# One wide operand for the high and low parts of the tokens in the single-stream projections

## The chip, the cores and the metric

The kernel runs on one core of a Trainium2 chip, in one launch. The metric is the device time of that core in microseconds (us), the median of several executions. Engines: PE is TensorE (PEld its weight loads), DVE is VectorE, ACT is ScalarE, POOL is GpSimd, SP is SyncE, which issues most of the DMAs.

## The reference

One layer of a hybrid block over 256 latent tokens and 256 context tokens, model width 2048, all in float32. What matters here are the matrix products of the latent tokens alone:

```python
hl = modulate(rmsnorm(x_lat, norm_mix[l]), m_lat[0], m_lat[1])
pl = hl @ w_in[l]                      # columns U, V, P, Q, O, K, VM, G
ql = silu(centred_dwconv(pl[Q]))       # 3 taps along the tokens, per channel
h_l = mlstm_bidir(ql, kl, vl, gl, ctx_states)            # 4 heads, 2 directions
y_b = sigmoid(pl[O]) * (rmsnorm of h_l * mlstm_norm)
y_a = gelu(pl[U]) * (spatial gating of gelu(pl[V]))
x_lat = x_lat + m_lat[2] * (concat(y_a, y_b, y_c) @ w_out[l])
hf = modulate(rmsnorm(x_lat, norm_ffn[l]), m_lat[3], m_lat[4])
q = hf @ peer_wq[l]                    # scores against keys, top 16, then the expert tables
x_lat = x_lat + m_lat[5] * peer_ffn(hf, ...)
out = rmsnorm(x_lat, norm_final)
```

The context tokens only pass through the columns K, VM and G.

## The kernel before

**Products in three parts.** A float32 weight tile `raw` is split in two: ACT copies it to `hi` in the rounded type fp32r (L282), and DVE takes the rest, `lo = raw - hi` (L292). The tokens are split in the same way, part 0 high and part 1 low, in the tiles `xL` (latent), `xC` (context), `ysplit` and `hf`. A product is hi x high + hi x low + lo x high, three matmuls into one PSUM tile.

**Units.** Weights come in units of 128 x 1024 (512 KB), half of a projection of 128 output channels. Each unit takes 8 of the 16 slices k of the model width (`add_cm`, L475). For one stream of 256 tokens that is 24 matmuls a unit, in the order (hi, 0), (hi, 1), (lo, 0) for every k, each with 256 columns. There are 52 such projections with one stream, 104 units, 832 slices: 8 of q, 8 of o, 4 of u, 16 of w_out and 16 of wq. K and the gates (two streams) and VM, V and P (`add_tm`, 512 columns) are made in other ways. Later, the 256 units of the table u_t (`u_use`, L323) pass `hA`, 192 tokens with high and low side by side, as one operand of 384 columns, then lo with 192.

**Order.** Everything is issued in program order by a planner in the kernel: `step` (L356) takes the next unit; `prepare` issues loads, `hi` and `lo` as far as slots are free (3 tiles of hi, 3 of lo); `flush` issues the evacuation (`q_done`, `o_done`, `u_done`, `o2_done`, `q2_done`) of the projection that ended one unit earlier; then come the unit's own matmuls. After the fourth k of a unit and after the unit, `pump` lets side work advance whose due time on a rough clock has come: lane "main" (states `gen_C` with the PSUM tile pc, then `gen_heads`), lane "score", and others. For lane "main" the due time also depends on the kernel's estimates of how far DVE and ACT have come. Each engine works off its own instructions in the order issued.

**Evacuation.** `conv_silu` (L677) for q: ACT copies PSUM to x, ACT scales it by the middle tap into y, DVE adds the two outer taps (two `scalar_tensor_tensor`, written big<-big,vecs 128x255), ACT does Silu and a last scaling. `o_done` and `u_done` read PSUM with one ACT activation; `o2_done` reads it with one DVE `scalar_tensor_tensor` onto the residual `x1`; `q2_done` with one ACT copy. Between units DVE also sums the condition's weights (`ada_use`, L434, adacc, 1024 columns).

**Heads.** For each head and direction, `weights` needs a broadcast from PE (bc), DVE (big<-bc, qw, sT) and an ACT Exp; `products` needs sT on PE (num, den); then den, diag, PE all, ACT E, and so on.

Of the kernel before, what the change touches and what calls it, by code (L numbers as in the profile page):

```python
# [32 lines left out]
P = 128  # L33
D = 2048
KD = D // P
T = 256
# [137 lines left out]
def build(tc, a, stack, dbg=None):  # L174
# [294 lines left out]
                add(a["ada2"][g - 2, part, k], False, ada_use(g, part, k))  # L469


    xL = A.tile([P, 2, KD, T], F32R, name="xL", tag="xL")
    xC = A.tile([P, 2, KD, T], F32R, name="xC", tag="xC")

    def add_cm(src, streams, done, n_ada=0):  # L475


        box = {}

        def use(half):  # L480
            def f(u):
                if half == 0:
                    box["ps"] = mm_ps()
                ps = box["ps"]
                xs = streams() if callable(streams) else streams
                hi = u.hi.rearrange("p (k c) -> p k c", c=P)
                lo = u.lo.rearrange("p (k c) -> p k c", c=P)
                for kt in range(8):
                    k = half * 8 + kt
                    for w, part in ((hi, 0), (hi, 1), (lo, 0)):  # L490
                        for n, x in enumerate(xs):
                            mm(ps[:, n * T:(n + 1) * T], w[:, kt], x[:, part, k],
                               start=(k == 0 and w is hi and part == 0 and n == 0),
                               stop=(k == KD - 1 and w is lo and n == len(xs) - 1))
                    if kt in MID:
                        pump()
                if half == 1:
                    post.append(lambda: done(ps))
            return f

        def put(half):
            add(src[:, half], True, use(half))
            add_ada(n_ada)
        return put
# [169 lines left out]
        yield 2.0  # L674


    def conv_silu(ps, ch, n):  # L677
        x, y = big()[:, 0:n], big()[:, 0:n]
        act.activation(x.rearrange("p n t -> p (n t)"), ps[:, 0:n * T], AF.Copy)

        def w(j):
            return vecs[:, V_CONV + j * 16 + ch:V_CONV + j * 16 + ch + 1]

        act.activation(y, x, AF.Copy, scale=w(1))
        vec.scalar_tensor_tensor(y[:, :, 1:], x[:, :, :T - 1], w(0), y[:, :, 1:], op0=OP.mult, op1=OP.add)
        vec.scalar_tensor_tensor(y[:, :, :T - 1], x[:, :, 1:], w(2), y[:, :, :T - 1], op0=OP.mult, op1=OP.add)
        return y
# [63 lines left out]
    def o_done(c):  # L751
        def f(ps):

            act.activation(V["yb"][:, c], ps[:, 0:T], AF.Sigmoid)
            act.activation(V["yb"][:, c], V["yb"][:, c], AF.Copy, scale=vecs[:, V_MLN + c:V_MLN + c + 1])
            V["o"] = c
        return f
# [186 lines left out]

    def u_done(c):
        def f(ps):
            act.activation(V["ya"][:, c], ps[:, 0:T], GELU)
            drain(only=("sgu",))
            ya = V["ya"][:, c].rearrange("p (b t) -> p b t", b=2)
            vec.tensor_tensor(ya, ya, mx[c], op=OP.mult)  # L950
        return f
# [23 lines left out]
    def finish_mix(u):  # L975
        drain(only=("main", "sgu", "pool"))
        dump("ya", V["ya"])
        dump("yb", V["yb"])
        dump("yc", V["yc"])
        y = Y["y"] = A.tile([P, 2, KD, T], F32R, name="ysplit", tag="xL")  # L980

        def v(k):
            q, c = divmod(k, 4)
            return (V["yc"][:, c], V["yb"][:, c], V["ya"][:, c], V["yb"][:, 4 + c])[q]

        skew(KD, lambda k: act.activation(y[:, 0, k], v(k), AF.Copy),
             lambda k: vec.tensor_tensor(y[:, 1, k], v(k), y[:, 0, k].bitcast(F32), op=OP.subtract))
        Y["x"] = A.tile([P, KD, T], F32, name="x1", tag="xc")
        load_x(0)
# [5 lines left out]
    def o2_done(c):  # L995
        def f(ps):
            x1 = Y["x"]
            vec.scalar_tensor_tensor(x1[:, c], ps[:, 0:T], mod[:, 2, 0, c:c + 1], x1[:, c],
                                     op0=OP.mult, op1=OP.add)
            if c % 4 == 0 and c + 4 < KD:  # L1000
                load_x(c // 4 + 1)
            sq = V["B"].tile([P, T], F32, name="sq1", tag="kc", bufs=2)
            act.activation(sq, x1[:, c], AF.Square)
            if c == KD - 1:

                warm = V["B"].tile([P, 1], F32, name="warm")
                act.activation(warm, ones[:, 0:1], AF.Sqrt)
                Y["last"] = sq
                return

            if c == 0:
                Y["sq"] = V["B"].tile([P, T], F32, name="sqs", tag="E")
            late.append(lambda: vec.tensor_copy(Y["sq"], sq) if c == 0 else
                        vec.tensor_tensor(Y["sq"], Y["sq"], sq, op=OP.add))
        return f
# [8 lines left out]
    def make_hf(u):  # L1024
        drain(only=("ada",))
        x1 = Y["x"]
        ss = mm_ps("ss1")
        mm(ss[:, 0:T], ones, Y["sq"], start=True, stop=False)
        mm(ss[:, 0:T], ones, Y["last"], start=False, stop=True)
        prepare()  # L1030
        rs = con.tile([P, T], F32, name="rs1", tag="rs1")
        rstd_of(rs, ss[:, 0:T], D)
        araws.drop(V["B"])
        close_pool(V["pb"])
        R["rh"] = open_pool("rh", side="right")
        R["rsb"] = open_pool("rsb", side="right")
        R["rs"] = open_pool("rs", side="right")
        H, S, SB = R["rh"][1], R["rs"][1], R["rsb"][1]
        hA = H.tile([P, KD, 2, NA], F32R, name="hA", tag="hA")
        hB = H.tile([P, D], F32, name="hB", tag="hB")  # L1040
        hf = A.tile([P, 2, KD, T], F32R, name="hf", tag="xC")
        R.update(hA=hA, hB=hB, hf=hf)
        R["keys"] = S.tile([P, 2, NK], F32, name="keys")
        sync.dma_start(R["keys"], a["keys"])
        sync.dma_start(x1d, x1)
        dump("x1", x1)
        n2 = 2 * PH * TOPK
        R["val"] = SB.tile([P, 2, n2], F32, name="val")
        R["ix"] = SB.tile([P, 2, n2], U32, name="ix")
        R["s0"] = SB.tile([P, 2 * PH, NK], F32, name="s0")  # L1050
        R["sc"] = SB.tile([P, PH, TOPK], F32, name="sc")
        R["ci"] = SB.tile([P, PH, TOPK], U32, name="ci")
        R["e12"] = SB.tile([P, 3, PH, TOPK], F32, name="e12")
        late = A.tile([P, 8192], F32, name="late", tag="xL")
        h32 = R["h32"] = late[:, 0:4096].rearrange("p (k t) -> p k t", t=T)
        R["scr"] = late[:, 4096:]
        spawn("hA", copy_hA())
        shift = mod[:, 3, 0]
        skew(KD,
             lambda k: vec.scalar_tensor_tensor(h32[:, k], x1[:, k], gm[:, 2, k:k + 1], rs,  # L1060
                                                op0=OP.mult, op1=OP.mult),
             lambda k: act.activation(hf[:, 0, k], h32[:, k], AF.Identity, bias=shift[:, k:k + 1]),
             lambda k: vec.scalar_tensor_tensor(hf[:, 1, k], h32[:, k], shift[:, k:k + 1],
                                                hf[:, 0, k].bitcast(F32), op0=OP.add, op1=OP.subtract))
        dump("hf", hf.bitcast(F32))

    hBd = tc.dram_tile([P, D], F32, name="hB_spill")

# [107 lines left out]
    def q2_done(hp):  # L1176
        def f(ps):
            S = R["rs"][1]
            at_most(1, "score")
            q = S.tile([P, T], F32, name="q2", tag="q2", bufs=2)  # L1180
            act.activation(q, ps[:, 0:T], AF.Copy)

            def g():
                yield 2.0
                pk = sm_ps("sc")
                for blk in range(2):
                    mm(pk[:, blk * P:(blk + 1) * P], q[:, blk * P:(blk + 1) * P], R["keys"][:, hp % 2],
                       start=True, stop=True)
                s = S.tile([P, NK], F32, name="s", tag="s", bufs=4)
                act.activation(s, pk[:, P:T], AF.Copy)  # L1190
                act.activation(R["s0"][:, hp], pk[:, 0:P], AF.Copy)
                R[hp] = s
                yield 1.5
                if hp % 2:
                    score_top(1, (hp - 1, R.pop(hp - 1)), (hp, R.pop(hp)))
                yield 0.0
                if hp % 4 == 3:
                    pair_top(1, hp // 2 - 1)
                    yield 0.0
                if hp == LOOK_AT:  # L1200
                    spawn("look", gen_look(1, 0, LOOK_Y))
            spawn("score", g())
        return f
# [523 lines left out]
```

## Time and profile before

| | |
|---|---|
| median of 3 executions | 1967.14 us (1966.36 to 1968.19) |
| profiled execution | 1964.81 us, span 1962.7 us |
| PE, PEld busy | 1727.7 us (88%), 1366.7 us (70%) |
| DVE, ACT busy | 1227.2 us (63%), 709.0 us (36%) |
| mean granted TensorE clock | 0.944 |
| HBM | 340 GB/s over the span |

Times in rows are microseconds from the start of the span. In the timeline, a matmul's first number is its start and the second its duration with the pipeline's filling and draining, so the distance between starts, not the duration, tells the pace. By the starts of the rows, the stages are: products with two streams to 183, VM to 281, q 283 to 337, o, V, P, o and u from 339 to 523 with the heads between them, w_out 532 to 630, wq 637 to 752, the table u_t from 753 on, and then the gathered rows of the table v.

### The profile page before, as it was taken

How to read it: one execution, taken by the hardware profiler on the slowest of the kernel's cores; microseconds unless marked ns; L12 is line 12 of the kernel's file. 1: busy time of each engine (PE TensorE's matmuls, PEld its weight loads, DVE VectorE, ACT ScalarE, POOL GpSimd, SP SyncE). 2: the span in 40 equal slices, each digit the busy share in tenths (PEclk: the TensorE clock that was granted, in tenths of full speed). 3: DMA queues.
4: the chain of work that ended last, by engine and by line, in shares of the span. 5: the costliest groups of instructions: out<-in, count | busy, mean ns of one | idle time of the engine just before them, and what ended most of it. 6: DMA issues, size and time to landing. Idle time of an engine off the chain costs nothing.

```text
span 1962.7 us, 30021 instructions
## 1 busy us (share of the span) xinstructions
PE 1727.7 (88%) x11882; PEld 1366.7 (70%) x11882; DVE 1227.2 (63%) x2504; ACT 709.0 (36%) x1131; POOL 376.1 (19%) x324
## 2 busy tenths in 40 slices
PE   4999999999898999899899999999987776767775
PEld 2689789979798998899789888888753222222221
DVE  5256868776798669899689998664434323323232
ACT  4236335555544654454434444444421001001010
POOL 0000000000000000333222323113333333333331
PEclk8999999999899999999999999999988889888887
DMA  9975878776598455999999999989989999999996
GB/s 397 375 268 181 289 245 305 273 250 205 197 348 291 150 177 197 409 420 420 418 350 406 396 395 393 357 343 408 377 345 421 421 420 421 420 421 422 420 421 288
DMA packets 115869, 670.20 MB, mean 341 GB/s; under 512 B 12688, under 2 KB 15248, under 8 KB 53264
## 3 DMA queue, kind: packets, MB, share of 16 engines
q1 hardware_dynamic: 69648, 332.72, 45.5%
q0 software_dynamic: 46080, 335.56, 41.8%
q8 instruction: 93, 1.52, 0.3%
q14 instruction: 48, 0.39, 0.1%
HBM read 662.99 MB, written 5.24 MB: 340 GB/s over the span
## 4 chain that ended last, share of the span: by engine, by line
PE 60%; DMA 26%; issue 5%; DVE 5%; ACT 2%; POOL 1%; SPq 0%; POOLq 0%; ACTq 0%; DVEq 0%
PE mm L345 25%; PE ups L345 22%; DMA gath<-in_v_rows,eA 7%; DMA rawB<-in_v_rows,eA 4%; DMA raw<-in_v_rows,eA 3%; PE adaps L345 3%; DMA hB<-in_v_rows,eA 2%; PE y L345 2%; DMA ring<-in_ada 2%; DMA rawB<-in_u_t 2%; DVE lo L130 2%; DMA rawA<-in_v_rows,eA 2%; PE sm L345 1%; PE num L345 1%; PE yb L345 1%
## 5 line engine op out<-in xcount | busy, mean ns | idle before, releaser
L345 PE MATMUL ups<-hA,hi 128*128 128x384 f32 x2048 | 607.2, 368 | 3.4 <-ACT hi L130 3.4
L345 PE MATMUL ups<-hA,lo 128*128 128x192 f32 x2048 | 518.8, 253 | 22.6 <-DVE lo L130 21.9
L345 PEld LDWEIGHTS ups<-hA,hi 128*128 128x128 f32 x2048 | 389.8, 190 | 53.3 <-issue 43.6
L345 PEld LDWEIGHTS ups<-hA,lo 128*128 128x128 f32 x2048 | 396.6, 194 | 27.6 <-DVE lo L130 27.4
L130 DVE TENSOR_TENSOR lo<-rawA,hi 128x1024 fp32r<-128x1024 f32 x158 | 192.7, 1221 | 120.8 <-ACT hi L130 106.0
L130 DVE TENSOR_TENSOR lo<-rawB,hi 128x1024 fp32r<-128x1024 f32 x156 | 190.3, 1221 | 116.3 <-ACT hi L130 108.3
L130 DVE SCALAR_TENSOR_TENSOR px<-c,iT,pick 128x128 f32<-128x128 f32 x192 | 55.3, 344 | 298.4 <-PE pick L345 289.8
L130 ACT ACTIVATE hi<-rawA 128x1024 fp32r<-128x1024 f32 x158 | 166.8, 1056 | 189.9 <-PE ups L345 91.3
L130 ACT ACTIVATE hi<-rawB 128x1024 fp32r<-128x1024 f32 x156 | 164.6, 1056 | 171.3 <-PE ups L345 68.4
L1351 POOL DMA_INDIRECT W<-in_u_rows,idx x30 | 48.7, 1623 | 894.2 <-PE ups L345 782.7
L345 PE MATMUL mm<-xL,hi 128*128 128x256 f32 x864 | 181.6, 290 | 4.8 <-ACT xL L130 1.7
L345 PEld LDWEIGHTS mm<-xL,hi 128*128 128x128 f32 x864 | 144.5, 193 | 14.2 <-issue 7.5
L130 DVE SCALAR_TENSOR_TENSOR adacc<-araw,early,adacc 128x1024 f32<-128x1024 f32 x120 | 152.3, 1277 | 0.0
L345 PE MATMUL y<-gath,wA 128*32 128x512 f32 x648 | 102.6, 720 | 53.2 <-DMA gath<-in_v_rows,eA 52.8
L130 ACT ACTIVATE uA<-uA 128x4 f32<-128x4 f32 x48 | 9.9, 206 | 385.8 <-DVE px L130 385.8
L130 ACT ACTIVATE hi<-W 128x1024 fp32r<-128x1024 f32 x82 | 86.9, 1059 | 107.3 <-PE ups L345 90.3
L345 PE MATMUL mm<-xL,lo 128*128 128x256 f32 x432 | 122.7, 284 | 0.0
L345 PEld LDWEIGHTS pick<-W,oh 128*128 128x128 f32 x384 | 79.7, 258 | 57.7 <-issue 56.2
L130 DVE TENSOR_TENSOR lo<-W,hi 128x1024 fp32r<-128x1024 f32 x82 | 99.4, 1218 | 15.2 <-ACT hi L130 13.5
L1351 POOL DMA_INDIRECT gath<-in_v_rows,idx x48 | 71.0, 1480 | 184.4 <-PE yb L345 90.4
L345 PE MATMUL mm<-hf,hi 128*128 128x256 f32 x512 | 100.0, 295 | 6.1 <-ACT hf L130 5.2
L1351 POOL DMA_INDIRECT gath<-in_v_rows,eA x81 | 76.6, 945 | 136.3 <-PE y L345 122.4
(291 smaller groups left out, 2985.2 us busy)
## 6 DMA issues: line engine op xcount, KB each, us to landing
araw<-in_ada SPq DMA_DIRECT2D x128, 512.0 KB, 5.3
W<-in_u_t SPq DMA_DIRECT2D x41, 1024.0 KB, 10.3
rawB<-in_u_t SPq DMA_DIRECT2D x40, 1024.0 KB, 11.3
rawA<-in_u_t SPq DMA_DIRECT2D x40, 1024.0 KB, 7.9
ring<-in_ada SPq DMA_DIRECT2D x32, 1024.0 KB, 11.8
rawB<-in_wout SPq DMA_DIRECT2D x16, 512.0 KB, 6.8
rawA<-in_wout SPq DMA_DIRECT2D x16, 512.0 KB, 5.7
rawB<-in_wq SPq DMA_DIRECT2D x16, 512.0 KB, 3.8
```

Of the source, the lines that this page charges most:

```text
L130: return f(*args, **kw)
L345: ten.matmul(out, lhsT, rhs, start=start, stop=stop, skip_group_check=True, **kw)
L1351: pool.indirect_dma_start(out=g.raw, out_offset=None, in_=tab, in_offset=bass.IndirectOffsetOnAxis(ap=idx, axis=0))
```

## The change

The token tiles `xL`, `ysplit` and `hf` now hold high and low of a slice k side by side. Where `add_cm` has one stream, hi is multiplied with both parts in one matmul of 512 columns, whose halves go to the two halves of the PSUM tile, and lo with the high part into the first half. The two halves are added when the tile is evacuated: `total` copies the second half on ACT and adds the first on DVE. q, o, u and wq use `total`; w_out adds each half onto the residual in an instruction of its own.

```diff
-    xL = A.tile([P, 2, KD, T], F32R, name="xL", tag="xL")
+    xL = A.tile([P, KD, 2, T], F32R, name="xL", tag="xL").rearrange("p k s t -> p s k t")
...
-                    for w, part in ((hi, 0), (hi, 1), (lo, 0)):
+                    if len(xs) == 1:
+                        mm(ps.rearrange("p (s t) -> p s t", s=2), hi[:, kt], xs[0][:, :, k], start=(k == 0), stop=False)
+                        mm(ps[:, 0:T], lo[:, kt], xs[0][:, 0, k], start=False, stop=(k == KD - 1))
+                    for w, part in ((hi, 0), (hi, 1), (lo, 0)) if len(xs) > 1 else ():
...
+    def total(dst, ps):
+        act.activation(dst, ps[:, T:2 * T], AF.Copy)
+        vec.tensor_tensor(dst, dst, ps[:, 0:T], op=OP.add)
+
     def conv_silu(ps, ch, n):
         x, y = big()[:, 0:n], big()[:, 0:n]
-        act.activation(x.rearrange("p n t -> p (n t)"), ps[:, 0:n * T], AF.Copy)
+        if n == 1:
+            total(x[:, 0], ps)
+        else:
+            act.activation(x.rearrange("p n t -> p (n t)"), ps[:, 0:n * T], AF.Copy)
...
-            act.activation(V["yb"][:, c], ps[:, 0:T], AF.Sigmoid)
+            total(V["yb"][:, c], ps)
+            act.activation(V["yb"][:, c], V["yb"][:, c], AF.Sigmoid)
...
-            act.activation(V["ya"][:, c], ps[:, 0:T], GELU)
+            total(V["ya"][:, c], ps)
+            act.activation(V["ya"][:, c], V["ya"][:, c], GELU)
...
-            vec.scalar_tensor_tensor(x1[:, c], ps[:, 0:T], mod[:, 2, 0, c:c + 1], x1[:, c],
-                                     op0=OP.mult, op1=OP.add)
+            for part in range(2):
+                vec.scalar_tensor_tensor(x1[:, c], ps[:, part * T:(part + 1) * T], mod[:, 2, 0, c:c + 1], x1[:, c],
+                                         op0=OP.mult, op1=OP.add)
...
-            act.activation(q, ps[:, 0:T], AF.Copy)
+            total(q, ps)
```

`ysplit` and `hf` change their layout as `xL` does.

On DVE, in the stage of q, this is the place of one projection's evacuation (big<-big,mm is the add of `total`, big<-big,vecs x2 the two outer taps, lo the next unit's weights):

```order
-L130 TENSOR_TENSOR lo_2431<-rawB,hi_2429 128x1024
+L130 TENSOR_TENSOR lo_2415<-rawB,hi_2413 128x1024
+L130 TENSOR_TENSOR big<-big,mm 128x256
 L130 SCALAR_TENSOR_TENSOR big<-big,vecs 128x255 x2
 L130 SCALAR_TENSOR_TENSOR adacc<-araw_2307,early,adacc 128x1024
 L130 COPY early<-pc 128x1 x2
```

The add stands between lo and the taps, and ACT's scaling of its result stands between the add and the taps.

On ACT, in the same stage, the evacuation of a state (b_1025<-pc) and the next units' hi; big<-big is the Silu, b_2361 the finished q:

```order
-L130 ACTIVATE hi_2719<-rawA 128x1024
-L130 ACTIVATE b_1025<-pc 128x256 x2
-L130 ACTIVATE hi_2761<-rawB 128x1024
+L130 ACTIVATE hi_2651<-rawA 128x1024
+L130 ACTIVATE hi_2675<-rawB 128x1024
 L130 ACTIVATE big<-mm 128x256
 L130 ACTIVATE big<-big,vecs 128x256
 L130 ACTIVATE big<-big 128x256
 L130 ACTIVATE b_2361<-big 128x256
-L130 ACTIVATE hi_2807<-rawB 128x1024
-L130 ACTIVATE hi_2839<-rawA 128x1024
+L130 ACTIVATE b_1025<-pc 128x256 x2
+L130 ACTIVATE hi_2719<-rawB 128x1024
+L130 ACTIVATE hi_2748<-rawA 128x1024
```

The copies of pc have moved from behind a hi to ahead of the next one; this happens twice in the stage.

On DVE, after the last projection of q, the weights of the first head (big<-bc, qw, sT):

```order
 L130 STREAM_TRANSPOSE adatr<-adat 128x256
 L130 TENSOR_TENSOR mod<-adatr,vecs 128x8
 L130 SCALAR_TENSOR_TENSOR gm<-mod,vecs 128x8
-L130 SCALAR_TENSOR_TENSOR big<-bc_3053,early 128x128
-L130 TENSOR_SCALAR big<-bc_3053,early 128x128
-L130 SCALAR_TENSOR_TENSOR big<-bc_3053,early 128x128
-L130 TENSOR_TENSOR qw<-b_2361,bc_3053 128x256 x2
+L130 TENSOR_TENSOR lo_2927<-rawA,hi_2925 128x1024
+L130 SCALAR_TENSOR_TENSOR adacc<-araw_2789,early,adacc 128x1024
+L130 SCALAR_TENSOR_TENSOR big<-bc_2941,early 128x128
+L130 TENSOR_SCALAR big<-bc_2941,early 128x128
+L130 SCALAR_TENSOR_TENSOR big<-bc_2941,early 128x128
+L130 TENSOR_TENSOR qw<-b_2361,bc_2941 128x256 x2
 L130 TENSOR_TENSOR sT<-big,S 128x256
 L130 TENSOR_TENSOR sT<-big,S 128x128
```

A lo and an adacc that stood behind sT now stand ahead of big<-bc. On PE, the first products num stand three units after the last unit of q, where they stood two and a half units after it.

## Rows read from the trace of the kernel before

**Rows 1.** The page's chain that ended last, by engine.
```profile
PE 60%; DMA 26%; issue 5%; DVE 5%; ACT 2%; POOL 1%; SPq 0%; POOLq 0%; ACTq 0%; DVEq 0%
```

**Rows 2.** Busy time by windows (length, engines, clock, DMA share, GB/s): q, w_out, wq.
```profile
281.00:343.00 62.00, 60.37 (x468) 57.36 (x467) 52.97 (x80) 36.50 (x64) 0.00 (x0) 1.00 0.84 291
...
532.00:631.00 99.00, 97.37 (x797) 95.44 (x798) 89.11 (x113) 42.58 (x63) 0.00 (x0) 0.97 0.82 304
637.00:753.00 116.00, 114.31 (x1085) 109.33 (x1085) 82.80 (x274) 65.45 (x133) 0.00 (x0) 0.97 0.47 161
```

**Rows 3.** Timeline (start, duration) of PE in w_out, 256 columns.
```profile
576.34 0.28 PE L345 MATMUL mm<-ysplit,lo 128*128 128x256 f32 x1
...
576.70 0.28 PE L345 MATMUL mm<-ysplit,lo 128*128 128x256 f32 x1
```

**Rows 4.** Timeline of PE in VM, 512 columns, first and last of 19.
```profile
209.84 0.39 PE L345 MATMUL mm<-hi,xC 128*128 128x512 f32 x1
...
213.92 0.39 PE L345 MATMUL mm<-hi,xL 128*128 128x512 f32 x1
```

**Rows 5.** Timeline of PE in u_t, 384 and 192 columns by turns.
```profile
757.18 0.36 PE L345 MATMUL ups<-hA,hi 128*128 128x384 f32 x1
757.38 0.25 PE L345 MATMUL ups<-hA,lo 128*128 128x192 f32 x1
757.47 0.36 PE L345 MATMUL ups<-hA,hi 128*128 128x384 f32 x1
```

**Rows 6.** Timeline of DVE in q; idle time and its releaser in brackets.
```profile
296.37 1.23 DVE L130 TENSOR_TENSOR lo<-rawB,hi 128x1024 fp32r<-128x1024 f32 x1 [0.79 <-ACT hi L130]
...
314.51 1.00 DVE L130 SCALAR_TENSOR_TENSOR big<-big,vecs 128x255 f32<-128x255 f32 x2
...
317.45 1.22 DVE L130 TENSOR_TENSOR lo<-rawA,hi 128x1024 fp32r<-128x1024 f32 x1 [0.74 <-ACT hi L130]
...
336.61 1.23 DVE L130 TENSOR_TENSOR lo<-rawB,hi 128x1024 fp32r<-128x1024 f32 x1 [0.75 <-ACT hi L130]
```

**Rows 7.** Timeline of ACT around the same projection of q.
```profile
312.05 0.51 ACT L130 ACTIVATE big<-big,vecs 128x256 f32<-128x256 f32 x1
315.60 0.42 ACT L130 ACTIVATE big<-big 128x256 f32<-128x256 f32 x1 [3.04 <-DVE big L130]
...
316.38 1.04 ACT L130 ACTIVATE hi<-rawA 128x1024 fp32r<-128x1024 f32 x1
```

**Rows 8.** Groups by form: a DVE tensor_tensor of 256 columns from PSUM.
```profile
L130 DVE TENSOR_TENSOR qw<-b,bc 128x256 f32<-128x256 f32 x16 | 5.9, 411 | 0.0
```

**Rows 9.** Timeline of DVE and PE at the first head.
```profile
343.73 0.35 DVE L130 SCALAR_TENSOR_TENSOR big<-bc,early 128x128 f32<-128x128 f32 x1 [0.69 <-PE bc L345]
...
345.18 0.62 DVE L130 TENSOR_TENSOR sT<-big,S 128x256 f32<-128x256 f32 x2
...
348.04 0.82 PE L345 MATMUL num<-sT,vlat 128*128 128x256 f32 x4
```

**Rows 10.** Timeline of ACT near the third head's norm.
```profile
486.96 1.28 ACT L130 ACT_TABLE_LOAD   x1
...
489.12 0.69 ACT L130 ACTIVATE diag<-c,hrs 128x128 f32<-128x128 f32 x2 [0.23 <-DVE hrs L130]
```

**Rows 11.** Timeline of PE there, and at the end of u.
```profile
489.70 0.66 PE L345 MATMUL all<-diag,ones 128*128 128x128 f32 x4
...
528.75 1.87 PE L345 MATMUL hss<-ones,h 128*128 128x1 f32 x8 [5.41 <-ACT h L130]
```

**Rows 12.** Timeline of DVE in w_out.
```profile
590.29 1.23 DVE L130 TENSOR_TENSOR lo<-rawB,hi 128x1024 fp32r<-128x1024 f32 x1 [0.28 <-ACT hi L130]
591.43 0.48 DVE L130 SCALAR_TENSOR_TENSOR x<-mm,mod,x 128x256 f32<-128x256 f32 x1
591.82 1.28 DVE L130 SCALAR_TENSOR_TENSOR adacc<-araw,early,adacc 128x1024 f32<-128x1024 f32 x1
```

**Rows 13.** Timeline of DVE and PE near the end of wq.
```profile
742.73 1.22 DVE L130 TENSOR_TENSOR lo<-rawA,hi 128x1024 fp32r<-128x1024 f32 x1
...
744.15 0.60 PE L345 MATMUL sc<-keys,q 128*128 128x128 f32 x4
```

**Rows 14.** Busy time by windows, around the end of u.
```profile
525.00:550.00 25.00, 18.50 (x125) 18.13 (x126) 18.71 (x34) 12.26 (x26) 0.00 (x0) 0.80 0.51 160
```

More of the change, by code (lines that the diff above doesn't have):

```diff
@@ L979, in finish_mix @@
         dump("yc", V["yc"])
-        y = Y["y"] = A.tile([P, 2, KD, T], F32R, name="ysplit", tag="xL")
+        y = Y["y"] = A.tile([P, KD, 2, T], F32R, name="ysplit", tag="xL").rearrange("p k s t -> p s k t")
         def v(k):
@@ L1040, in make_hf @@
         hB = H.tile([P, D], F32, name="hB", tag="hB")
-        hf = A.tile([P, 2, KD, T], F32R, name="hf", tag="xC")
+        hf = A.tile([P, KD, 2, T], F32R, name="hf", tag="xC").rearrange("p k s t -> p s k t")
         R.update(hA=hA, hB=hB, hf=hf)
@@ L1064, in make_hf @@
                                                 hf[:, 0, k].bitcast(F32), op0=OP.add, op1=OP.subtract))
-        dump("hf", hf.bitcast(F32))
+        dump("hf", hf)
     hBd = tc.dram_tile([P, D], F32, name="hB_spill")
```

## The prediction

> **What bounds the kernel now.** I read the chain of waits first: it runs over PE for most of the span and over DMA for the gathered rows at the end [rows 1]. The changed stages lie in front of that, so I went to the busy time by windows: in q, w_out and wq PE is busy nearly throughout at full clock, and DMA has room [rows 2]. So the pace of PE's matmuls counts there, as long as DVE and ACT keep up. DVE is close: 52.97 of 62.00 us in q and 89.11 of 99.00 in w_out. Then I read the timeline, where the distance between starts is the pace. Three matmuls of 256 columns take 0.36 us, 120 ns each [rows 3]; 18 steps of 512 columns take 4.08 us, 226.7 ns each [rows 4]. At 2.4 GHz the columns alone would need 106.7 and 213.3 ns, so every matmul costs 13.3 ns besides its columns.
>
> **PE.** A slice took 3 x 120 = 360 ns and will take 226.7 + 120 = 346.7: 13.3 ns less, 0.107 us a unit, 11.1 us over 832 slices. The neighbours are the pairs of 384 and 192 columns in u_t, 0.29 us a pair [rows 5], where 576 columns and two times 13.3 would be 267 ns; 20 ns are unexplained. If that is a price of alternating lengths, a slice costs 367 ns, 7 more than before. If it is because the load of the next weights outlasts the stream of 192 columns (80 ns), it vanishes here, since 256 columns take longer; the pair then lasts 340 to 347 ns. I take 346.7, with 340 and 367 as ends.
> The Trainium skill (TensorE: Matmul & The Clock Gate, section Back-to-back issue gap) gives columns / 2.4 + 2.5 ns for a matmul at full clock. By it a slice would gain 2.5 ns, and the sum below would be about 10.6 instead of 3.5. The trace's 13.3 ns decides. The same page (section LDWEIGHTS) puts a load of 128 columns at columns / 1.2, an estimated 107 ns; that is longer than 80 ns and supports the second reading of rows 5, and no row here separates the two.
>
> **q, 283 to 337.** Here PE is not alone. After the taps of one projection (314.51, done 315.5) ACT does Silu (315.60), the last scaling, and only then the next hi (316.38); DVE's lo waits for that hi, idle 0.74 us, until 317.45 [rows 6, 7]. That hi did not wait for PE. DVE and ACT form a ring whose time is spent on these two engines alone: from 296.37 to 336.61 it made 6 rounds, 6.71 us each [rows 6], which is also PE's pace (48 x 0.12 = 5.76 plus the matmuls of the states). In the round ACT's scaling by the middle tap is hidden: it ran at 312.05 to 312.56, two us before the taps [rows 7]. With the change it can't be. DVE's add stands between lo and the taps, and the scaling needs the add: 0.41 for the add [rows 8], 0.10 until ACT starts (as from 315.50 to 315.60), 0.51 for the scaling, 0.04 back: 1.06 us a round. The ring then needs 7.8 us where PE needs 6.5, so DVE and ACT set the pace. Over 8 projections that is 8.5 us. The copies of pc, 0.64 us, now stand ahead of a hi in two rounds and lengthen them: about 1.4. So the last taps come 9.9 us late. Next, a lo (1.14) and an adacc (1.19) have moved ahead of the first head's weights; they take the 0.69 us that DVE idled there and wait about half a microsecond for their hi: 9.9 + 2.3 - 0.7 + 0.6 = 12.1, so sT ends at 357.9 instead of 345.80 [rows 9]. PE needs sT for num, which had 2.24 us to spare (348.04) [rows 9] and now has none. num starts at 357.9, 9.9 later; PE will have done half a unit more by then, 1.4 us. Net **+8.5**, and PE's own gain in q is lost in this wait. The bounds: -1.7 if the ring does not bind and PE keeps its 16 x 0.107; +10 if the order brings still more.
>
> **The rest of o, and u.** 21 units x 0.107 = -2.2. ACT's copy, the wait for DVE's add and the activation now follow each other, about 0.4 us where a table load covers the wait. Of the heads' waits most have 1 us or more to spare. The one without is the third head's norm: diag ends at 489.81, after PE's start of all at 489.70 [rows 10, 11]. Ahead of it ACT will wait for lo and the add, some 1.4 us before the table load of 486.96 [rows 10]: +1.6. At the end of u, PE already waits 5.41 us for a chain over DVE and ACT [rows 11]; the last head's products stand later in the order and the adds ahead of the chain, -1 to +1, taken as 0. Net **-0.6**, bounds -2.2 and +3.
>
> **w_out.** The first unit runs at a lower clock (below) and gains nothing. 31 x 0.107 = -3.3. DVE gets a second x<-mm, whose distance to the next instruction is 0.39 [rows 12]. A round of DVE is 5.76 us with 0.37 us lost at the wait of 590.29 (0.28 in the row, the rest in handing over), so 5.39 of work; it becomes 5.78 against PE's 5.55. DVE falls behind by 0.24 us a projection; its lo is ready 3.1 us ahead, which lasts 13 projections, and the sums adacc end before the last two. So PE does not wait; the cover is gone if PE is faster than I think. The last projection's second add delays what follows: +0.4. Net **-2.9**, bounds -4 and 0.
>
> **wq.** 30 units x 0.107 = -3.2. q2 has one more hop, over DVE; sc uses it one and a half units later. That is enough but for one place: after the lo of 742.73 the add ends near 744.3, and sc ran at 744.15 [rows 13]. PE comes 2.9 us earlier, DVE 2.3 less one add: a wait of 1.1 to 1.4. From 750 DVE is busy without a break until the first gather, with one more add in it, +0.3. Net **-1.5**, bounds -3 and +1.
>
> From there every stage starts after the one before it, in the same order on all engines, so I carry the shift to the end.
>
> **Sum.** 8.5 - 0.6 - 2.9 - 1.5 = **+3.5 us**, on 1964.81 us of the profiled execution (1962.7 of span) 1968.3. The median is 2.33 above that execution, so I expect **1970.6**. About 0.2%, 3.9 us, is what can be told from no change.
>
> **Rivals.**
> A, the forecast, 0.37; its own range 1967.5 to 1974.
> B, the ring gives way: the order leaves DVE enough lead in q, and PE keeps its gain. For it: DVE is idle in q for 9 of 62 us [rows 2]. Against it: that idle time is inside the ring. About 100 units x 0.107 = -10.7, +0.4 after w_out, +1.4 in wq: 1958. 0.15.
> C, half of it: PE waits for lo in q (some 3.5 us more than before), but the first head's weights are not late. 3.5 - 0.6 - 2.9 - 1.5 = -1.5: 1965.6. 0.20.
> D, the wait costs clock as well. After the idle 5.41 us at 528.75 the granted clock of 525 to 550 was 0.80 on average [rows 11, 14], that is, 10 of 25 us at 1.2 GHz, of which some 5 us were idle. PE's wait for sT would be about 4 us in one piece, after shorter ones. 5 to 8 us of work at half clock cost 2.5 to 4: 1974. For it: the row; against it: the wait is shorter. 0.21. The Trainium skill (the same page, section on HAM oscillation) says that bursts with pauses between them start slow each time; the row agrees with it, and whether this pause is long enough no row shows.
> E, alternating lengths cost 20 ns as in rows 5: 82 units outside q at +0.16 each against the forecast, +13: 1984. It is slower from the first slice on. 0.07.
> That the change doesn't do what it says, I leave out: the order shows 832 matmuls of 512 columns in place of 1664.
>
> **Numbers.** Leaving out B and E, the range is 1960 to 1977. Faster by over 0.2% (under 1963.2): B and a little of C, 0.19. Slower by over 0.2% (over 1971.1): D, E and the upper part of A, 0.43. Within: 0.38.
>
> **What would show it.** In the changed profile: hi of 512 followed by lo at 0.227 us and the next hi 0.12 after it; in q, rounds of DVE near 7.8 us, with ACT's scaling after the add, and waits of PE for lo; before the first num a wait of PE for sT of several us; o's first units about 8 us late; w_out's units at 2.77 us instead of 2.88 and DVE without idle time; the start of u_t 3 to 4 us late. The forecast is wrong if q's rounds stay below 7 us (then B or C) or a slice takes other than 347 ns.

## The result, and the profile after

The changed kernel takes 1979.97 us (median of 5 runs, 1976.44 to 1982.4) against 1966.36 for the kernel before (5 runs, 1963.73 to 1968.19). The ratio is 1.007, with a 95% interval of 1.0057 to 1.0083: 13.8 us slower by the ratio (the medians differ by 13.6), where +3.5 was forecast and 1977 was the upper end of the range. The profiled execution has a span of 1978.2 us.

Where the time went is read from the starts of the same unit's first matmul in both timelines, each less the start of q's first unit (283.24 before, 282.95 after):

| stretch, up to the start of | before | after | lost in it | forecast |
|---|---|---|---|---|
| q: fourth unit of o | 354.08 | 362.90 | +9.1 | +8.5 |
| o, u: second unit of w_out | 539.35 | 548.72 | +0.5 | -0.6 |
| w_out: its last unit | 627.26 | 635.20 | -1.4 | -3.3 |
| end of w_out: second unit of wq | 644.10 | 655.05 | +3.0 | +0.4 |
| wq: first unit of u_t | 753.40 | 767.83 | +3.5 | -1.5 |
| u_t and the rest: end | 1962.7 | 1978.2 | +1.1 | 0 |

The stretches add up to 15.8 us. Less the 0.3 us by which q starts earlier, that is 15.5, the difference of the two profiled executions, and about 2 us more than that of the medians.

Busy time by windows (length, then PE, PEld, DVE, ACT, POOL with counts, clock, DMA share, GB/s) for q, w_out and wq after, beside [rows 2]:

```profile
281.00:347.00 66.00, 60.46 (x331) 49.55 (x330) 52.43 (x81) 33.55 (x59) 0.00 (x0) 1.00 0.81 259
541.00:640.00 99.00, 96.14 (x540) 81.12 (x538) 93.94 (x125) 41.19 (x62) 0.00 (x0) 0.96 0.83 301
648.00:768.00 120.00, 112.79 (x833) 93.68 (x834) 89.79 (x291) 65.26 (x133) 0.00 (x0) 0.97 0.48 158
```

In q and wq PE now stands still for 5.5 and 7.2 us, where it was 1.6 and 1.7; in w_out DVE has 93.94 us of work in 99, where it had 89.11.

**PE.** The timeline of PE in w_out (start, duration), to be set beside [rows 3]:

```profile
602.83 0.40 PE L345 MATMUL mm<-ysplit,hi 128*128 128x512 f32 x1
603.06 0.28 PE L345 MATMUL mm<-ysplit,lo 128*128 128x256 f32 x1
603.18 0.40 PE L345 MATMUL mm<-ysplit,hi 128*128 128x512 f32 x1
603.42 0.28 PE L345 MATMUL mm<-ysplit,lo 128*128 128x256 f32 x1
603.54 0.40 PE L345 MATMUL mm<-ysplit,hi 128*128 128x512 f32 x1
```

From hi to lo it is 0.23 to 0.24 us, from lo to hi 0.12, 0.35 to 0.36 a slice. In w_out most units take 2.81 to 2.84 us (353 ns a slice), in wq's shortest 2.77 (346). PE gains 7 to 14 ns a slice, not 13.3 throughout.

**q.** DVE and ACT in q after, beside [rows 6, 7] (idle time and its releaser in brackets):

```profile
312.98 1.23 DVE L130 TENSOR_TENSOR lo<-rawB,hi 128x1024 fp32r<-128x1024 f32 x1 [0.79 <-ACT hi L130]
...
317.10 0.41 DVE L130 TENSOR_TENSOR big<-big,mm 128x256 f32<-128x256 f32 x1
318.10 1.00 DVE L130 SCALAR_TENSOR_TENSOR big<-big,vecs 128x255 f32<-128x255 f32 x2 [0.58 <-ACT big L130]
319.01 1.28 DVE L130 SCALAR_TENSOR_TENSOR adacc<-araw,early,adacc 128x1024 f32<-128x1024 f32 x1
321.04 1.23 DVE L130 TENSOR_TENSOR lo<-rawA,hi 128x1024 fp32r<-128x1024 f32 x1 [0.74 <-ACT hi L130]
...
328.99 1.22 DVE L130 TENSOR_TENSOR lo<-rawB,hi 128x1024 fp32r<-128x1024 f32 x1 [0.79 <-ACT hi L130]
```

```profile
317.55 0.51 ACT L130 ACTIVATE big<-big,vecs 128x256 f32<-128x256 f32 x1 [3.38 <-DVE big L130]
319.19 0.42 ACT L130 ACTIVATE big<-big 128x256 f32<-128x256 f32 x1 [1.13 <-DVE big L130]
319.64 0.42 ACT L130 ACTIVATE b<-big 128x256 f32<-128x256 f32 x1
319.97 1.04 ACT L130 ACTIVATE hi<-rawA 128x1024 fp32r<-128x1024 f32 x1
```

Two rounds take 16.01 us (312.98 to 328.99): 8.0 each. The chain is complete in the rows: add 317.10, scaling 317.55, taps 318.10, Silu 319.19, hi 319.97, lo 321.04. PE waits inside q as well (engine, tile, releaser; us in total, times, longest), and before the first num:

```profile
PE mm L345 <- DVE lo L130: 2.1, 4, 0.8
...
PE mm L345 <- ACT hi L130: 1.2, 2, 1.0
PE adat L345 <- DVE early L130: 0.6, 1, 0.6
```

```profile
356.60 0.92 PE L345 MATMUL num<-sT,vlat 128*128 128x256 f32 x4 [2.58 <-DVE sT L130]
```

The wait for sT also cost clock. PE's windows around it (the granted clock stands third from the end):

```profile
350.00:356.00 6.00, 4.03 (x24) 3.23 (x22) 5.47 (x11) 4.22 (x7) 0.00 (x0) 1.00 0.78 244
356.00:358.00 2.00, 1.40 (x6) 1.26 (x7) 1.64 (x4) 1.98 (x4) 0.00 (x0) 0.85 0.68 186
358.00:360.00 2.00, 2.00 (x6) 1.55 (x6) 1.86 (x3) 1.57 (x3) 0.00 (x0) 0.50 0.82 277
```

num, which took from 348.04 to the first all at 355.52 before, 7.5 us, now takes from 356.60 to 365.81, 9.2. So q's loss adds up: num 8.85 late (corrected for the start), 1.4 back for the half unit that PE has done ahead of it, 1.7 for the clock, 9.15 in all.

**The end of w_out.** DVE and then PE, between the last matmul of w_out (638.21) and the first of wq:

```profile
639.10 1.23 DVE L130 TENSOR_TENSOR lo<-rawB,hi 128x1024 fp32r<-128x1024 f32 x1 [1.43 <-PE adat L345]
640.24 0.42 DVE L130 TENSOR_TENSOR sqs<-sqs,sq 128x256 f32<-128x256 f32 x1
640.58 0.99 DVE L130 SCALAR_TENSOR_TENSOR x<-mm,mod,x 128x256 f32<-128x256 f32 x2
...
643.15 1.23 DVE L130 TENSOR_TENSOR lo<-rawA,hi 128x1024 fp32r<-128x1024 f32 x1 [1.02 <-ACT hi L130]
```

```profile
640.80 0.67 PE L345 MATMUL ss<-sqs,ones 128*128 128x256 f32 x2 [1.74 <-DVE sqs L130]
642.13 0.70 PE L345 MATMUL ss<-sq,ones 128*128 128x256 f32 x2 [0.66 <-ACT sq L130]
648.80 0.77 PE L345 MATMUL mm<-hf,hi 128*128 128x512 f32 x1 [5.97 <-DVE hf L130]
```

Before, with the last matmul of w_out at 630.02:

```profile
630.33 0.48 DVE L130 SCALAR_TENSOR_TENSOR x<-mm,mod,x 128x256 f32<-128x256 f32 x1
...
637.31 1.23 PE L345 MATMUL mm<-hf,hi 128*128 128x256 f32 x2 [5.23 <-ACT hf L130]
```

The last addition onto the residual started 0.31 us after the start of PE's last matmul before (630.33); now it starts 2.37 us after it (640.58). DVE is late: a round of it in w_out takes 5.9 us where PE needs 5.66, as the additions onto the residual show, and between 568.10 and 639.10 no row of it has an idle time.

```profile
595.86 1.00 DVE L130 SCALAR_TENSOR_TENSOR x<-mm,mod,x 128x256 f32<-128x256 f32 x2
...
601.76 0.99 DVE L130 SCALAR_TENSOR_TENSOR x<-mm,mod,x 128x256 f32<-128x256 f32 x2
```

Ahead of the last addition stands a lo whose hi waited on ACT for the square of the addition before (the row of that lo names PE's adat; adat and that hi end at the same time, 639.06). Then the addition is two instructions, +0.5, and wq's first matmul needs the low part of hf, which DVE makes, where it needed the high part alone before: from the instruction behind that lo to wq's first matmul it is 648.80 - 644.29 = 4.51 against 3.77, +0.74. That is 2.06 + 0.5 + 0.74 = 3.3, and 0.25 for a wait inside the last unit; 0.5 come back in wq's first unit.

**wq.** DVE at its end, and the scores of the last projection on PE, beside [rows 13]:

```profile
764.24 1.20 DVE L130 TENSOR_TENSOR lo<-rawB,hi 128x1024 fp32r<-128x1024 f32 x1
765.37 1.21 DVE L130 TENSOR_REDUCE e<-late 128x64 f32<-128x1024 f32 x1
766.50 0.41 DVE L130 TENSOR_TENSOR q<-q,mm 128x256 f32<-128x256 f32 x1
```

```profile
766.96 1.21 PE L345 MATMUL sc<-keys,q 128*128 128x128 f32 x4 [2.75 <-DVE q L130]
```

ACT copied its half at 764.25, 0.3 us after the last matmul's start. The add of the other half waits in DVE's queue behind the top 16 of an earlier pair, a lo and a reduction. Before, ACT's copy alone released the scores:

```profile
752.93 0.71 PE L345 MATMUL sc<-keys,q 128*128 128x128 f32 x4 [0.53 <-ACT q L130]
```

The waits of sc for DVE's q sum to 4.7 us in wq, in three places.

### The profile page after: what moved, and what is told of

Read it like the earlier page. It is cut to its first block, busy times and chain, and to the rows that moved or that the text cites. A ratio compares the mean times of both kernels' runs of the same rounds, so it can differ in the third digit from the quotient of the medians.

```text
span 1978.2 us, 28398 instructions
## 1 busy us (share of the span) xinstructions
PE 1727.4 (87%) x11050; PEld 1320.6 (67%) x11050; DVE 1246.0 (63%) x2556; ACT 711.2 (36%) x1143; POOL 377.6 (19%) x324
## 4 chain that ended last, share of the span: by engine, by line
PE 27%; DMA 25%; issue 4%; DVE 4%; ACT 1%; POOL 1%; POOLq 0%; SPq 0%; ACTq 0%; DVEq 0%
PE ups L345 22%; DMA hB<-in_v_rows,eA 9%; DMA gath<-in_v_rows,eA 4%; DMA raw<-in_v_rows,eA 2%; DMA rawB<-in_v_rows,eA 2%; DMA rawB<-in_u_t 2%; PE y L345 2%; DMA rawA<-in_u_t 2%; DVE lo L130 2%; DMA rawA<-in_v_rows,eA 1%; PE adaps L345 1%; PE yb L345 1%; DVE W L130 1%; DMA hB<-hB_spill 1%; PE pick L345 1%
## 5 line engine op out<-in xcount | busy, mean ns | idle before, releaser
L345 PE MATMUL mm<-xL,hi 128*128 128x512 f32 (+1 forms) x544 | 179.3, 361 | 6.1 <-ACT xL L130 1.7
L345 PEld LDWEIGHTS mm<-xL,hi 128*128 128x128 f32 x544 | 104.2, 192 | 28.3 <-issue 7.1
L345 PE MATMUL mm<-hf,hi 128*128 128x512 f32 x256 | 96.1, 415 | 7.0 <-DVE hf L130 6.8
```

Source lines behind the costliest of these rows:

```text
L345: ten.matmul(out, lhsT, rhs, start=start, stop=stop, skip_group_check=True, **kw)
```

## The experiments

Theory 1: the matmuls gain, and the added adds cost more, because they stand in chains over DVE and ACT that PE waits for. Theory 2: the wide operand itself costs, or the planner's order. The table gives for each run the ratio to the kernel before on the same chip, whose medians there were 1964.24 to 1966.63 us, and what it lost by stage, worked out as above (q; o and u; w_out; its end; wq).

| run | ratio (95%) | q | o, u | w_out | end | wq |
|---|---|---|---|---|---|---|
| changed kernel | 1.007 (1.0057 to 1.0083) | +9.1 | +0.5 | -1.4 | +3.0 | +3.5 |
| wide, one half read | 0.9971 (0.9959 to 0.9983) | -1.2 | -1.3 | -2.9 | +0.1 | -2.3 |
| adds alone | 1.0092 (1.0078 to 1.0107) | +7.6 | +2.1 | +0.4 | +1.5 | +5.1 |
| q as before | 1.0031 (1.0017 to 1.0045) | -0.2 | +1.1 | -1.0 | +2.9 | +3.7 |
| q alone | 1.0048 (1.0035 to 1.0061) | +9.1 | +0.3 | 0.0 | -0.3 | +0.3 |
| w_out alone | 1.0005 (0.9992 to 1.0019) | 0.0 | +0.6 | -1.3 | +2.5 | +0.2 |
| wq alone | 1.0015 (1.0001 to 1.0029) | 0.0 | +0.1 | 0.0 | +0.2 | +3.4 |
| w_out and wq, adds to POOL | 1.0027 (1.0015 to 1.0039) | 0.0 | +0.5 | +0.3 | +2.9 | +2.2 |
| taps later | 1.0082 (1.0066 to 1.0099) | +11.1 | +0.7 | -1.4 | +3.0 | +3.2 |
| all three mended | 1.0059 (1.0045 to 1.0073) | +11.0 | +0.7 | +0.3 | +2.9 | -0.1 |
| Silu later | 1.0024 (1.0013 to 1.0034) | -0.4 | +0.4 | -1.4 | +3.0 | +3.6 |
| Silu later, narrow | 0.9991 (0.9979 to 1.0002) | 0.0 | +0.5 | +0.1 | -0.3 | +0.3 |
| selective | 0.9980 (0.9969 to 0.9992) | -0.2 | -0.2 | -1.0 | -0.3 | -0.6 |
| selective and q | 0.9988 (0.9975 to 1.0001) | -0.4 | -0.1 | -1.0 | -0.3 | -0.6 |

From u_t on, where no edit changes the code, the single profiles lose between -4.0 us (w_out and wq, adds to POOL) and +4.1 (selective and q) against the kernel before, and q starts up to 4 us earlier or later in them. So the stages say more than the ends, and the ratios rest on many executions.

**Matmuls and adds apart.** First, every evacuation reads one half, as in the kernel before:

```diff
...
-            total(q, ps)
+            act.activation(q, ps[:, 0:T], AF.Copy)
...
```

> All wide matmuls stay, but every evacuation reads only the first half of the PSUM tile, with the instructions that the kernel before had (the products hi x low are left out of the output). Theory 1, the adds cost the time (waits on DVE and ACT; the matmuls themselves win about 6.5 ns a slice, since the changed profile shows slices of 346 to 356 ns against 360): 832 x 6.5 ns = 5.4 us less than before, perhaps 0.7 given back because the first matmul of hf now needs the low part too: about 1961 to 1963 us. Theory 2, the wide operand itself costs (PE alternates lengths, needs both parts at once, loses clock): no better than 1975.

1958.4 us: 0.9971, 5.7 us less than before. The wide operand costs nothing, and the gain of 104 units shows in every stage of matmuls. In w_out 23 of its units take 2.77 us, the 347 ns a slice of the forecast, and the later ones 2.83; when w_out alone is wide (below), the pace changes from 2.83 to 2.77 and back within the stage. What chooses between the two paces, no run shows. Second, the adds without the wide matmuls:

```diff
-                        mm(ps.rearrange("p (s t) -> p s t", s=2), hi[:, kt], xs[0][:, :, k], ...)
-                        mm(ps[:, 0:T], lo[:, kt], xs[0][:, 0, k], ...)
+                        for w, part, n in ((hi, 0, 0), (hi, 1, 1), (lo, 0, 0)):
+                            mm(ps[:, n * T:(n + 1) * T], w[:, kt], xs[0][:, part, k], ...)
```

> Three matmuls of 256 columns as before, but hi x low into the second half of the PSUM tile, and the changed kernel's evacuation with its adds. Theory 1: as slow as the changed kernel or slower, since PE's gain is gone and the adds stay: 1980 to 1985. Theory 2 (the wide operand costs): the adds are hidden, 1966 to 1970.

1983.16: 1.0092, 18.1 us more. q loses 7.6 and wq 5.1 without a wide matmul. PE waits 2.09 us for sT here and keeps its clock, and q loses 1.5 us less than in the changed kernel, where the clock took 1.7. Theory 2 falls as far as it means the operand.

**By stages.** q goes back to three matmuls, then only q is wide (the flag is set per call of `add_cms`):

> The changed kernel with q's eight projections as before (three matmuls, one half). Theory 1: the ring of DVE and ACT in q costs about 9 us, which go: 1980 - 9 = 1971 (1969 to 1973), and PE's first num follows the last unit of q as before. Theory 2: 8 of 52 projections go back, at most 15% of the loss: 1977 to 1979. If the ring is there but the late start of the heads would be hidden later on: 1974 to 1977.

> The kernel before with only q's eight projections wide and added on evacuation. Theory 1: 1966 + 9 = 1975 (1973 to 1977), with PE's waits for lo in q. Theory 2: 1966 + 2 = 1968. If the parts do not add up (the later stages absorb a late start): below 1972.

1972.11 and 1973.55. q's 9.1 us go with it and come with it alone, and no later stage takes them up. By the ratios the first saves 13.8 - 6.1 = 7.7 us and the second costs 9.4; by stages it is 9.3 and 9.1.

> The kernel before with only w_out wide and its second addition onto the residual. Theory 1 (the lead of DVE is used up and the last addition comes late): PE's 30 units 1.4 us shorter, then about 3 us lost between the last matmul of w_out and the second unit of wq: +1.6 us against the kernel before (0 to +3). Theory 2 (that loss only follows from the late start of w_out in the changed kernel): -2 to -3.

1968.11, within noise of before. The stages answer: -1.3 and +2.5, although the second unit of w_out starts only 0.6 us late here, not 9.7. DVE at its end:

```profile
630.45 1.00 DVE L130 SCALAR_TENSOR_TENSOR x<-mm,mod,x 128x256 f32<-128x256 f32 x2
632.88 1.22 DVE L130 TENSOR_TENSOR lo<-rawB,hi 128x1024 fp32r<-128x1024 f32 x1 [1.43 <-PE adat L345]
634.02 0.42 DVE L130 TENSOR_TENSOR sqs<-sqs,sq 128x256 f32<-128x256 f32 x1
634.36 1.00 DVE L130 SCALAR_TENSOR_TENSOR x<-mm,mod,x 128x256 f32<-128x256 f32 x2
```

The same order with the same 1.43 us of idle time. So the loss belongs to w_out, and is not a consequence of its late start.

> The kernel before with only wq wide and added on evacuation as in the change. Theory 1: units 2.3 us shorter, waits of the scores for DVE's addition 1.6 + 0.5 + 0.9 + 2.6, of which u_t's early wait (4.2 us in its third unit before) absorbs 3.6 at most: -0.5 to +1.5 at the fourth unit of u_t, and +0.5 to +3 in all, since the changed kernel also lost 1 to 2 us in u_t. If wq is harmless alone: -2.5.

1969.11, and +3.4 up to u_t, as in the changed kernel. The wait before the last scores is there again:

```profile
756.20 0.71 PE L345 MATMUL sc<-keys,q 128*128 128x128 f32 x4 [2.80 <-DVE q L130]
```

**Mending it.** Additions to POOL: sqs by `pool.tensor_tensor`, and in wq

```diff
...
-            total(q, ps)
+            act.activation(both.rearrange("p s t -> p (s t)"), ps, AF.Copy)
+            pool.tensor_tensor(q, both[:, 0], both[:, 1], op=OP.add)
```

> Only w_out and wq wide. The sum of the squares (sqs) moves from DVE to POOL in w_out; in wq ACT copies both halves in one instruction and POOL adds them, so that no addition stands in DVE's queue. Theory 1: PE keeps its gain in both, -2.9 and -2.7, and gives back 0.7 where hf needs its low part: -4 to -5.5 against the kernel before. Theory 2 (the additions cost wherever they stand, or POOL slows DVE down): -1 to +2.

1970.32, by the ratio 5.3 us more than before: outside both ranges, theory 2 nearer. What DVE and POOL do in w_out suggests the reason, which no further run tests:

```profile
592.64 1.38 DVE L130 TENSOR_TENSOR lo<-rawA,hi 128x1024 fp32r<-128x1024 f32 x1 [0.30 <-ACT hi L130]
```

```profile
591.80 1.14 POOL L1025 TENSOR_TENSOR sqs<-sqs,sq 128x256 f32<-128x256 f32 x1 [4.99 <-ACT sq L130]
```

sqs had filled the time in which the next hi was made; without it DVE idles 0.30 us there. And a lo that starts beside POOL's add takes 1.38 us instead of 1.21. The round of 6.12 us is longer than 5.9. In wq POOL's add takes 0.7 to 1.7 us, and PE waits 3.4 us for it.

Then q's taps, Silu and scaling, one step later:

```diff
+            def finish():
+                taps()
+                act.activation(y[:, 0], y[:, 0], AF.Silu)
...
+                late.append(finish)
```

> The changed kernel; in q the taps, the Silu and the last scaling of a projection are issued one unit after its addition (the last projection's at once), so that DVE does not wait 0.58 us for ACT's scaling and ACT's hi does not wait for the taps of the same unit. Theory 1 (the ring): rounds of q near 7 us instead of 8.0, 4 to 7 us less than the changed kernel: 1973 to 1976. Theory 2 (DVE's instructions alone fill the round, or the order of the planner costs): within 2 us of the changed kernel.

1979.95: by the ratios 2.4 us more than the changed kernel, and q loses 11.1 instead of 9.1. This was my mistake about the place. DVE after this edit:

```profile
301.17 0.99 DVE L130 SCALAR_TENSOR_TENSOR big<-big,vecs 128x255 f32<-128x255 f32 x2
304.11 1.23 DVE L130 TENSOR_TENSOR lo<-rawA,hi 128x1024 fp32r<-128x1024 f32 x1 [1.94 <-ACT hi L130]
```

The 0.58 us went, but adacc now stands ahead of the taps and no longer covers taps, Silu, hi, lo: 1.94 us idle instead of 0.74, and 8.0 us a round again; the wait before the first num grew from 2.58 to 3.44 us. The ring has to be cut, not shortened at one wait.

> The changed kernel with all three: taps of q a unit later, sqs on POOL, addition of wq on POOL. Theory 1: q +3, o and u +0.5, w_out -2, wq -2.5 against the kernel before: -1, between -3 and +2. Theory 2: 1975 or more.

1976.49: the three edits together, as theory 2 had it. By stages wq gains 3.6 us on the changed kernel; q and w_out lose 1.9 and 1.7. POOL's adds in wq, which cost +2.2 above, cost nothing here (-0.1): PE waits 2.0 us for them instead of 3.4. What decides that is open.

So only the Silu and the last scaling are put behind the next hi (two steps later), taps and add stay:

```diff
+    def defer(n, f):
+        late.append(f if n == 1 else lambda: defer(n - 1, f))
...
+            if c < 7:
+                defer(2, finish)
```

> The changed kernel; in q the addition, scaling and taps stay where they are, but the Silu and the last scaling on ACT (which wait for the taps) are issued behind the next hi. Theory 1 (the ring taps, Silu, hi, lo): ACT's hi no longer waits for the taps; DVE's round is what its instructions and the 0.58 us wait for the scaling add up to, about 6.9 us instead of 8.0: five rounds x 1.1 = 5 us less than the changed kernel, 1973 to 1976. Theory 2 (DVE's work or the place of the heads sets q): within 1.5 us of the changed kernel.

> The kernel before (three matmuls of 256, no additions) with the same later place of Silu and scaling: the control of the run above. Theory 1: PE already sets the pace of q there, so -1 to +0.5 us. If the gain above comes from the order alone and not from the ring that the addition tightens: -4 or more here too.

1970.2 and 1964.85. By the ratios the first is 9.0 us faster than the changed kernel, and q's loss is gone in full. DVE in q:

```profile
309.99 0.41 DVE L130 TENSOR_TENSOR big<-big,mm 128x256 f32<-128x256 f32 x1
310.98 1.00 DVE L130 SCALAR_TENSOR_TENSOR big<-big,vecs 128x255 f32<-128x255 f32 x2 [0.58 <-ACT big L130]
...
323.92 0.41 DVE L130 TENSOR_TENSOR big<-big,mm 128x256 f32<-128x256 f32 x1
```

Two rounds in 13.93 us, 6.97 each, as expected; the 0.58 us are still there and do not matter. I had counted the shorter rounds alone. With them most of the wait for sT goes too, and the clock stays at 1.00 behind it:

```profile
352.69 0.92 PE L345 MATMUL num<-sT,vlat 128*128 128x256 f32 x4 [0.71 <-DVE sT L130]
```

The lo and the adacc that the change moved ahead of the first head's weights still stand there (348.44 and 349.58, ahead of big<-bc at 350.77). So that move of the planner's order is not by itself what q lost by. The control, the kernel before with the same order, stands at 0.9991 (0.9979 to 1.0002), no change that can be told: it is the add that made the ring bind.

**A version that beats both.** Wide only where the rows show the add hidden:

```diff
+O1, WO, WQ = True, (1, 2, 3, 4, 5, 6, 7), (1, 2, 3, 5, 6, 7, 8, 10, 12)
...
+            if hp in WQ:
+                total(q, ps)
+            else:
+                act.activation(q, ps[:, 0:T], AF.Copy)
```

> Wide only where theory 1 finds the addition hidden: the first four projections of o, projections 1 to 7 of w_out (DVE regains its lead after them), and 1, 2, 3, 5, 6, 7, 8, 10 and 12 of wq (not those whose addition meets a long job of DVE, nor the first and the last). 8 + 14 + 18 units x 8 x 9.5 ns = 3.0 us less than the kernel before, and no wait in its place: -2 to -3.5. Theory 2 (any addition costs): 0 or slower.

1962.11: 0.9980 (0.9969 to 0.9992), by the ratio 3.9 us faster than before, and faster than the changed kernel. It loses in no stage, and is 2.3 us ahead at the start of u_t.

> The selective kernel (wide in the first half of o, in projections 1 to 7 of w_out and in nine of wq) and q wide too, with its Silu and last scaling behind the next hi. If the ring was all that q lost by, PE keeps its gain there: 1 us less than the selective kernel, 4 to 5 less than the kernel before in all. If q's rounds only just keep up (6.96 us against 6.71) and the heads start later: no gain over the selective kernel, or 1 to 2 us lost.

1964.17, 0.9988 (0.9975 to 1.0001), 2.4 us less than before and not told from the run above. The second reading holds: PE is 1.1 us ahead at the start of o and gives most of it back, since sT comes late still:

```profile
347.12 0.92 PE L346 MATMUL num<-sT,vlat 128*128 128x256 f32 x4 [0.72 <-DVE sT L131]
```

## Why the prediction was wrong

The direction and the largest cause were right, the size was not: +13.8 us instead of +3.5. Two terms of the sum failed: what follows w_out, put at +0.4 and measured at +3.0, and the waits of wq, put at +1.7 and measured at 4.7 us. Of the cases on record only E (1984) lies beyond the result, by a mechanism that no run shows.

- **q, the mechanism right, the number partly luck.** +9.1 against +8.5, a round of 8.0 us against 7.8, and the chain add, scaling, taps, Silu, hi, lo as forecast. But two misses offset each other: sT ended 1 us earlier than forecast, and the clock took 1.7, which the term did not have.
- **PE, half of the size.** The slice was taken as 346.7 ns. It is 346 to 356 in the changed kernel, near 353 in w_out: from a wide matmul to the narrow one behind it 0.23 to 0.24 us pass instead of 0.227. In w_out's 30 units that is 30 x 8 x 6.3 ns = 1.5 us. The rule of the Trainium skill that was weighed there (TensorE: Matmul & The Clock Gate, section Back-to-back issue gap; 2.5 ns for each matmul saved, an estimated 2.1 us over 832 slices) is too small, though: with one half read, the matmuls alone gained 5.7.
- **w_out: "So PE does not wait", and +0.4 for what follows.** PE indeed hardly waits: some 0.2 us in the third unit from the end, 0.25 in the last. The lag of DVE was forecast at 0.24 us a projection, and 5.9 us a round against 5.66 bear it out, by luck: both were taken too short, 5.78 and 5.55 (the second addition costs DVE 0.5 us a projection and not 0.39). The step that failed is the +0.4: the lead covers PE, but at the end DVE's lateness delays the last addition and all that follows from it: +3.0. That the first matmul of hf needs the low part (0.74 of it) was not seen at all.
- **wq: "That is enough but for one place".** The add was weighed by its own 0.41 us and not by what stands ahead of it in DVE's queue. PE waited 4.7 us in three places, the longest at the last projection, where "+0.3" was put: -1.5 became +3.5. At the one place that was named, the scores came without a wait (756.01, the place of 744.15 before).
- **o and u.** The wait before the third head's all is there, 1.18 us (498.96 in PE's timeline) where 1.6 was added. The last heads' products half a unit later cost about what the units gain: +0.5 instead of -0.6.
- **Rivals.** D came true in part: the clock fell after the wait for sT, for 1.7 us and not 2.5 to 4. What the Trainium skill says of bursts with pauses that start slow (TensorE: Matmul & The Clock Gate, section on HAM oscillation) fits that row. B and C had the ring giving way; E had the slice at 367 ns, and no run shows that. No rival had the end of w_out or wq on the losing side, and the upper bounds of those two terms, 0 and +1, were too tight. That is why the result lay above the range.

Shown by runs: q's ring, w_out's end, wq's adds, PE's gain. Of the split at the end of w_out, the +0.74 and the -0.5 are borne out by the run with one half read, which has these two alone (4.51 us from that instruction to wq's first matmul, and +0.1 for the whole stretch). Argued from rows only: the rest of that split, and the cost of the half unit at the last heads. Open: the last 1.1 us from u_t on, which is within the scatter there.

## What to carry to other kernels

An add on evacuation costs what stands ahead of it in its engine's queue and what its consumer can wait, not its own 0.4 us; write the chain from the add to the next matmul that needs it, stage by stage, the last unit of each stage above all. When two engines hand work back and forth, cut the loop by moving the instruction that the next round waits behind (here the Silu behind the next hi), since removing one wait in it moves the idle time elsewhere. And a stage whose helper engine is slower than PE by a quarter of a microsecond a round can pay for it at its end: here the last addition came 2.1 us later against PE's last matmul, although PE had hardly waited before.

## What the hardware showed besides

PE at full clock waited 1.18 us (498.96) and 1.63 us (before the scores at 696.29), and the granted clock stayed at 1.00 in the windows behind. After 2.58 us before num, after 2.75 before the last scores, and in the kernel before after 2.46 in u_t, it fell to 0.50, that is 1.2 GHz. The windows behind the last scores:

```profile
764.00:766.00 2.00, 0.21 (x2) 0.00 (x0) 2.00 (x5) 0.38 (x1) 0.00 (x0) 1.00 0.00 0
766.00:768.00 2.00, 1.04 (x5) 1.04 (x6) 1.11 (x3) 0.00 (x0) 0.00 (x0) 0.75 0.77 197
768.00:770.00 2.00, 2.00 (x9) 2.00 (x9) 1.48 (x11) 1.39 (x3) 0.00 (x0) 0.50 0.81 336
```

u_t's first unit took 3.55 us there instead of 2.35.

The length of the last wait alone does not tell what the clock does. In other runs PE at full clock kept 1.00 after 2.09 us (adds alone, before num) and 2.42 us (selective and q, 756.55 in u_t), and fell to 0.50 after 2.12 us (q alone, 769.46 in u_t). At the end of w_out the same wait of 1.74 us for sqs left the clock at 1.00 in the changed kernel (640.80), and in the run with q as before it fell within 2 us (635.41).
